# A residual layer norm: the last eight blocks of rows in smaller chunks, without their gamma and beta passes

## The chip, the cores and the metric

The kernel runs on one core of one Trainium2 chip. The metric is the device time in microseconds (us); a lower time is better. The page of the profile shows one execution, and its span is a little shorter than the device time of the same run.

Five engines matter here, and they run side by side. VectorE is DVE in the profile, ScalarE is ACT, GpSimd is POOL. SyncE is SP; it only issues loads. POOL only issues the loads of gamma and beta and the stores of the output. TensorE has no work. Transfers between the chip's main memory and the on-chip memory are done by 16 DMA engines.

## The reference

```python
def setup_inputs():
    batch, seq, dim = 16, 1024, 512
    return {
        "x": np.random.randn(batch, seq, dim).astype(np.float32),
        "residual": np.random.randn(batch, seq, dim).astype(np.float32),
        "gamma": np.ones(dim, dtype=np.float32),
        "beta": np.zeros(dim, dtype=np.float32),
        "eps": np.float32(1e-5),
    }

def reference(x, residual, gamma, beta, eps):
    z = x + residual
    mean = np.mean(z, axis=-1, keepdims=True)
    var = np.var(z, axis=-1, keepdims=True)
    z_norm = (z - mean) / np.sqrt(var + eps)
    return (gamma * z_norm + beta).astype(np.float32)
```

There are 16,384 rows of 512 numbers. A block is 128 rows, one row to each partition of the on-chip memory, so there are 128 blocks. The inputs x and residual are 33.6 MB each, and so is the output. Gamma is all ones and beta all zeros.

## The kernel before

Each of 32 chunks has R = 4 blocks: two loads of 1 MB, and one output of 1 MB. The code has two halves. `produce` starts the loads of a chunk and works out its statistics; `consume` normalizes the chunk before it and stores it. The framework orders the instructions of each engine when the kernel is built, and it may move them a little against the order of the source.

```python
R = 4
BUFS = 8
ACT_APPLY = (0, 2)
PIPE_DEPTH = 1
# ... cut: shapes, pools, the loads of gamma and beta ...

    def produce(st):
        base = st * rows_super
        # ... cut: x_ap and r_ap, the rows of this chunk; a partition gets r_cur rows that lie together
        xt = data.tile([P, r_cur, D], FP32, name="xt")
        rt = data.tile([P, r_cur, D], FP32, name="rt")
        ot = data.tile([P, r_cur, D], o_dt, name="ot")
        nc.sync.dma_start(out=xt[:], in_=x_ap)
        nc.sync.dma_start(out=rt[:], in_=r_ap)
        # ... cut: S and Qc
        for n in range(r_cur):                       # DVE: z = x + residual, and its row sums S
            nc.vector.tensor_tensor_reduce(
                out=xt[:, n, :], in0=xt[:, n, :], in1=rt[:, n, :],
                scale=1.0, scalar=0.0, op0=ALU.add, op1=ALU.add,
                accum_out=S[:, n : n + 1],
            )
        nmean = stats.tile([P, r_cur], FP32, name="nmean")
        nc.scalar.mul(nmean[:], S[:], -inv_D)        # ACT: the negative mean
        for n in range(r_cur):                       # ACT: the sum of squares of z - mean
            nc.scalar.activation(
                out=junk[:], in_=xt[:, n, :], func=AF.Square,
                bias=nmean[:, n : n + 1], accum_out=Qc[:, n : n + 1],
            )
        # ... cut: std = sqrt(Qc / D + eps) on ACT, rstd = 1 / std and nmr = nmean * rstd on DVE
        return dict(st=st, xt=xt, ot=ot, nmean=nmean, rstd=rstd, nmr=nmr)

    def consume(c):
        # ... cut
        for n in range(r_cur):                       # two blocks of four on ACT, two on DVE
            if n in ACT_APPLY:
                nc.scalar.activation(
                    out=ot[:, n, :], in_=xt[:, n, :], func=AF.Identity,
                    bias=nmr[:, n : n + 1], scale=rstd[:, n : n + 1],
                )
            else:
                nc.vector.tensor_scalar(
                    out=ot[:, n, :], in0=xt[:, n, :],
                    scalar1=nmean[:, n : n + 1], scalar2=rstd[:, n : n + 1],
                    op0=ALU.add, op1=ALU.mult,
                )
        nc.vector.tensor_mul(ot[:], ot[:], g_b)      # DVE: gamma, in fp16
        nc.vector.tensor_add(ot[:], ot[:], b_b)      # DVE: beta, in fp16
        nc.gpsimd.dma_start(out=o_ap, in_=ot[:])     # POOL: the store, fp16 to fp32 on the way

    for st in range(n_super):
        state.append(produce(st))
        if st >= PIPE_DEPTH:
            consume(state[st - PIPE_DEPTH])
    # ... cut: consume of the last chunk
```

A load waits until the load eight before it has landed, which the framework adds. `ot` is fp16, and the store turns it into fp32.

Of the kernel before, what the change touches and what calls it, by code (L numbers as in the profile page):

```python
# [1 line left out]

# [4 lines left out]

FP32 = mybir.dt.float32
FP16 = mybir.dt.float16  # L10
AF = mybir.ActivationFunctionType
ALU = mybir.AluOpType

R = 4
BUFS = 8
FP16_CHAIN = True
ACT_APPLY = (0, 2)
PIPE_DEPTH = 1


@with_exitstack
def kernel(
    ctx: ExitStack,
    tc: tile.TileContext,
    x: bass.AP,
    residual: bass.AP,
    gamma: bass.AP,
    beta: bass.AP,
    eps: bass.AP,
    out: bass.AP,  # L30
):
    nc = tc.nc
    P = nc.NUM_PARTITIONS

    x_f = x.flatten_outer_dims()
    r_f = residual.flatten_outer_dims()
    o_f = out.flatten_outer_dims()
    N, D = x_f.shape
    inv_D = 1.0 / float(D)
    eps_val = float(eps)  # L40

    r_cur = R
    while N % (P * r_cur) != 0 and r_cur > 1:
        r_cur -= 1
    rows_super = P * r_cur
    n_super = N // rows_super

    o_dt = FP16 if FP16_CHAIN else FP32

    consts = ctx.enter_context(tc.tile_pool(name="consts", bufs=1))  # L50
    data = ctx.enter_context(tc.tile_pool(name="data", bufs=BUFS))
    stats = ctx.enter_context(tc.tile_pool(name="stats", bufs=BUFS))
    psum = ctx.enter_context(tc.tile_pool(name="psum", bufs=1, space=bass.MemoryType.PSUM))

    g_t = consts.tile([P, D], o_dt, name="g_t")
    b_t = consts.tile([P, D], o_dt, name="b_t")
    nc.gpsimd.dma_start(out=g_t[:], in_=gamma.partition_broadcast(P))  # L57
    nc.gpsimd.dma_start(out=b_t[:], in_=beta.partition_broadcast(P))  # L58
    eps_t = consts.tile([P, 1], FP32, name="eps_t")
    nc.vector.memset(eps_t[:], eps_val)  # L60
    junk = psum.tile([P, D], FP32, name="junk")

    g_b = g_t[:].unsqueeze(1).to_broadcast((P, r_cur, D))
    b_b = b_t[:].unsqueeze(1).to_broadcast((P, r_cur, D))

    state = []

    def produce(st):
        base = st * rows_super
        x_ap = x_f[base : base + rows_super].rearrange("(p n) d -> p n d", n=r_cur)  # L70
        r_ap = r_f[base : base + rows_super].rearrange("(p n) d -> p n d", n=r_cur)

        xt = data.tile([P, r_cur, D], FP32, name="xt")
        rt = data.tile([P, r_cur, D], FP32, name="rt")
        ot = data.tile([P, r_cur, D], o_dt, name="ot")
        nc.sync.dma_start(out=xt[:], in_=x_ap)  # L76
        nc.sync.dma_start(out=rt[:], in_=r_ap)  # L77

        S = stats.tile([P, r_cur], FP32, name="S")
        Qc = stats.tile([P, r_cur], FP32, name="Qc")  # L80

        for n in range(r_cur):
            nc.vector.tensor_tensor_reduce(  # L83
                out=xt[:, n, :],
                in0=xt[:, n, :],
                in1=rt[:, n, :],
                scale=1.0,
                scalar=0.0,
                op0=ALU.add,
                op1=ALU.add,  # L90
                accum_out=S[:, n : n + 1],
            )
        nmean = stats.tile([P, r_cur], FP32, name="nmean")
        nc.scalar.mul(nmean[:], S[:], -inv_D)  # L94
        for n in range(r_cur):
            nc.scalar.activation(  # L96
                out=junk[:],
                in_=xt[:, n, :],
                func=AF.Square,
                bias=nmean[:, n : n + 1],  # L100
                accum_out=Qc[:, n : n + 1],
            )
        std = stats.tile([P, r_cur], FP32, name="std")
        nc.scalar.activation(  # L104
            out=std[:], in_=Qc[:], func=AF.Sqrt, bias=eps_t[:], scale=inv_D
        )
        rstd = stats.tile([P, r_cur], FP32, name="rstd")
        nc.vector.reciprocal(out=rstd[:], in_=std[:])  # L108
        nmr = stats.tile([P, r_cur], FP32, name="nmr")
        if ACT_APPLY:  # L110
            nc.vector.tensor_mul(nmr[:], nmean[:], rstd[:])  # L111
        return dict(st=st, xt=xt, ot=ot, nmean=nmean, rstd=rstd, nmr=nmr)

    def consume(c):
        st, xt, ot = c["st"], c["xt"], c["ot"]
        nmean, rstd, nmr = c["nmean"], c["rstd"], c["nmr"]
        base = st * rows_super
        o_ap = o_f[base : base + rows_super].rearrange("(p n) d -> p n d", n=r_cur)
        for n in range(r_cur):
            if n in ACT_APPLY:  # L120
                nc.scalar.activation(  # L121
                    out=ot[:, n, :],
                    in_=xt[:, n, :],
                    func=AF.Identity,
                    bias=nmr[:, n : n + 1],
                    scale=rstd[:, n : n + 1],
                )
            else:
                nc.vector.tensor_scalar(  # L129
                    out=ot[:, n, :],  # L130
                    in0=xt[:, n, :],
                    scalar1=nmean[:, n : n + 1],
                    scalar2=rstd[:, n : n + 1],
                    op0=ALU.add,
                    op1=ALU.mult,
                )
        nc.vector.tensor_mul(ot[:], ot[:], g_b)  # L137
        nc.vector.tensor_add(ot[:], ot[:], b_b)  # L138
        if FP16_CHAIN:
            nc.gpsimd.dma_start(out=o_ap, in_=ot[:])  # L140
        else:
            nc.scalar.dma_start(out=o_ap, in_=ot[:])

    for st in range(n_super):
        state.append(produce(st))
        if st >= PIPE_DEPTH:
            consume(state[st - PIPE_DEPTH])
            state[st - PIPE_DEPTH] = None
    for st in range(n_super - PIPE_DEPTH, n_super):
        if state[st] is not None:  # L150
            consume(state[st])


# [1 line left out]
_INS = ['x', 'residual', 'gamma', 'beta', 'eps']  # L155
_OUTS = [((16, 1024, 512), 'float32')]
#: Inputs that are plain numbers.
_NUMBERS = {'eps': 9.999999747378752e-06}


# [26 lines left out]
```

## Time and profile before

| What | Number |
|---|---|
| Device time, median of 4 runs | 258.94 us |
| Lowest and highest | 258.68 and 258.95 us |
| Span on the page | 257.2 us |
| Moved by DMA | 101.01 MB, mean 393 GB/s |
| Loads of x and residual, median from issue to landing | 29.6 and 30.0 us |
| Outputs, median from issue to landing | 9.3 us |

Busy time alone does not tell what bounds a kernel, since the engines work side by side and a stretch near the end may have another limit than the rest. The page has slices in time for that, and the trace can be asked for the busy time in any stretch, and for its single instructions. The names in a line of the profile are those of the code: `xt<-xt,rt` is the addition, `junk<-xt,nmean` the squares, `ot<-xt,nmr,rstd` the normalizing on ACT, `ot<-xt,nmean,rstd` that on DVE, `ot<-ot,g_t` and `ot<-ot,b_t` the passes of gamma and beta.

### The profile page before, as it was taken

To read this page: it belongs to the slowest core of one execution; us is meant where nothing else is said; L and a number is where in the kernel's file an instruction comes from. 1 tells how busy PE (TensorE), PEld (TensorE's weight loads), DVE (VectorE), ACT (ScalarE), POOL (GpSimd) and SP (SyncE) were. 2 spreads that over 40 slices of the span, in tenths; PEclk is the share of its full clock that TensorE was granted. 3 is DMA by queue.
4 is the path that set the end of the run, shared out by engine and by line. 5 is a ranking of instruction groups with operands and counts; after the bars stand their busy time and mean duration, and the time that the engine had idled before them with its cause. 6 is when DMAs were issued, how large, how long until landed. Compare 5 with 4: busy or idle time off the path is not lost.

```text
span 257.2 us, 1160 instructions
## 1 busy us (share of the span) xinstructions
DVE 193.1 (75%) x449; ACT 164.7 (64%) x386; POOL 18.4 (7%) x38
## 2 busy tenths in 40 slices
DVE  0357999588877787977977798777879779679860
ACT  1188788575765677656767766557776567576640
POOL 2000000000000000000000000000000000000000
DMA  7999999999999999999999999999999999996444
GB/s 259 312 426 427 419 427 418 420 426 427 424 419 424 424 423 420 423 424 427 420 422 423 426 424 420 423 424 423 420 424 423 426 422 420 423 426 260 163 163 163
DMA packets 14121, 101.01 MB, mean 393 GB/s; under 512 B 1568, under 2 KB 1824, under 8 KB 1824
## 3 DMA queue, kind: packets, MB, share of 16 engines
q1 hardware_dynamic: 9216, 67.11, 67.8%
q0 software_dynamic: 4896, 33.82, 33.4%
q14 instruction: 9, 0.07, 0.1%
HBM read 67.63 MB, written 33.55 MB: 393 GB/s over the span
## 4 chain that ended last, share of the span: by engine, by line
DMA 91%; issue 2%; ACT 2%; SPq 1%; DVE 1%; POOLq 0%; DVEq 0%
DMA rt<-in_residual_dram 91%; ACT junk L96 1%; DVE xt L83 1%; SPq L76 1%; SPq L77 1%; ACT ot L121 1%; POOLq L182 0%; ACT std L104 0%; ACT nmean L94 0%; DVE rstd L108 0%; DVE nmr L111 0%; DVE S L83 0%; DVEq L83 0%
## 5 line engine op out<-in xcount | busy, mean ns | idle before, releaser
L83 DVE CUSTOM_DVE_ANT_0 xt<-xt,rt 128x512 f32<-128x512 f32 x128 | 84.4, 680 | 47.5 <-DMA rt<-in_residual_dram 47.5
L121 ACT ACTIVATE ot<-xt,nmr,rstd 128x512 f16<-128x512 f32 x64 | 51.4, 806 | 67.3 <-DVE nmr L111 67.3
L96 ACT ACTIVATE junk<-xt,nmean 128x512 f32<-128x512 f32 x128 | 87.9, 687 | 3.1
L137 DVE TENSOR_TENSOR ot<-ot,g_t 128x2048 f16<-128x2048 f16 x32 | 39.2, 1225 | 6.7 <-ACT ot L121 6.6
L138 DVE TENSOR_TENSOR ot<-ot,b_t 128x2048 f16<-128x2048 f16 x32 | 39.2, 1224 | 1.1
L140 POOL DMA_DIRECT2D out_dram<-ot x32 | 17.0, 532 | 231.9 <-DVE ot L138 192.3
L129 DVE TENSOR_SCALAR ot<-xt,nmean,rstd 128x512 f16<-128x512 f32 x64 | 31.9, 540 | 0.0
L96 ACT ACTIVATION_READ_ACCUMULATOR junk<-xt,nmean 128x1 f32 x128 | 23.9, 186 | 0.0
L94 ACT ACTIVATE nmean<-S 128x4 f32<-128x4 f32 x32 | 6.1, 190 | 11.0 <-DVE S L83 11.0
L83 DVE DVE_READ_ACCUMULATOR2_ANT S<- 128x1 f32 x128 | 10.4, 82 | 0.0
L104 ACT ACTIVATE std<-Qc,eps_t 128x4 f32<-128x4 f32 x32 | 9.5, 297 | 1.0
L108 DVE RECIPROCAL rstd<-std 128x4 f32<-128x4 f32 x32 | 5.5, 172 | 1.1 <-ACT std L104 1.1
L111 DVE TENSOR_TENSOR nmr<-nmean,rstd 128x4 f32<-128x4 f32 x32 | 5.0, 157 | 0.0
L94 ACT ACT_TABLE_LOAD x1 | 1.3, 1283 | 0.7 <-PEq L168 0.7
L104 ACT ACT_TABLE_LOAD x1 | 1.3, 1283 | 0.0
L57 POOL DMA_DIRECT2D g_t<-in_gamma_dram x1 | 0.7, 669 | 0.8 <-PEq L182 0.8
L60 DVE MEMSET eps_t<- 128x1 f32 x1 | 0.1, 59 | 0.8 <-PEq L168 0.8
L58 POOL DMA_DIRECT2D b_t<-in_beta_dram x1 | 0.5, 540 | 0.0
L168 POOL MEMSET const-float32-0.0<- 128x1 f32 x1 | 0.1, 98 | 0.2 <-issue 0.2
L168 POOL MEMSET const-bfloat16-1.0<- 128x1 bf16 x1 | 0.1, 101 | 0.0
L168 POOL MEMSET const-float32-1.0<- 128x1 f32 x1 | 0.1, 98 | 0.0
L168 POOL MEMSET const-uint8-127<- 128x1 uint8 x1 | 0.1, 98 | 0.0
## 6 DMA issues: line engine op xcount, KB each, us to landing
xt<-in_x_dram SPq DMA_DIRECT2D x32, 1024.0 KB, 29.6
rt<-in_residual_dram SPq DMA_DIRECT2D x32, 1024.0 KB, 30.0
out_dram<-ot POOLq DMA_DIRECT2D x32, 1024.0 KB, 9.3
g_t<-in_gamma_dram POOLq DMA_DIRECT2D x1, 128.0 KB, 9.5
b_t<-in_beta_dram POOLq DMA_DIRECT2D x1, 128.0 KB, 12.2
```

The source lines that it names most:

```text
L76: nc.sync.dma_start(out=xt[:], in_=x_ap)
L83: nc.vector.tensor_tensor_reduce(out=xt[:, n, :], in0=xt[:, n, :], in1=rt[:, n, :], scale=1.0, scalar=0.0, op0=ALU.add, op1=ALU.add, accum ...
L94: nc.scalar.mul(nmean[:], S[:], -inv_D)
L96: nc.scalar.activation(out=junk[:], in_=xt[:, n, :], func=AF.Square, bias=nmean[:, n : n + 1], accum_out=Qc[:, n : n + 1],)
L104: nc.scalar.activation(out=std[:], in_=Qc[:], func=AF.Sqrt, bias=eps_t[:], scale=inv_D)
L108: nc.vector.reciprocal(out=rstd[:], in_=std[:])
L111: nc.vector.tensor_mul(nmr[:], nmean[:], rstd[:])
L121: nc.scalar.activation(out=ot[:, n, :], in_=xt[:, n, :], func=AF.Identity, bias=nmr[:, n : n + 1], scale=rstd[:, n : n + 1],)
L129: nc.vector.tensor_scalar(out=ot[:, n, :], in0=xt[:, n, :], scalar1=nmean[:, n : n + 1], scalar2=rstd[:, n : n + 1], op0=ALU.add, op1=ALU. ...
L137: nc.vector.tensor_mul(ot[:], ot[:], g_b)
L138: nc.vector.tensor_add(ot[:], ot[:], b_b)
L140: nc.gpsimd.dma_start(out=o_ap, in_=ot[:])
```

## The change

The first 120 blocks still go in 30 chunks of four. The last eight go in chunks of 2, 2, 1, 1, 1 and 1 instead of two of four, so that less work is left to do once the last load has landed. There are nine buffers instead of eight. ACT normalizes the first half of a chunk's blocks, rounded; for a chunk of one block that is `round(0.5)`, which is 0 in Python, so DVE does it.

One more thing changes in the code: the passes of gamma and beta run only where a chunk has four blocks. For the last eight blocks they are left out. With gamma all ones and beta all zeros the numbers stay the same, but for other values of gamma and beta the last 1,024 rows would be without them. The times are to be read with this in mind.

```diff
-R = 4
-BUFS = 8
+BODY_R = 4
+HEAD_CHUNKS = []
+TAIL_CHUNKS = [2, 2, 1, 1, 1, 1]
+BUFS = 9
-ACT_APPLY = (0, 2)
-PIPE_DEPTH = 1
+ACT_APPLY_FRAC = 0.5
+DUAL_QUEUE_LOADS = False
 ... (cut: the list of chunks is made from these)
-        xt = data.tile([P, r_cur, D], FP32, name="xt")
-        nc.sync.dma_start(out=xt[:], in_=x_ap)
-        nc.sync.dma_start(out=rt[:], in_=r_ap)
+        xt = data.tile([P, BODY_R, D], FP32, name="xt")
+        nc.sync.dma_start(out=xt[:, 0:r_cur, :], in_=x_ap)
+        (nc.scalar if DUAL_QUEUE_LOADS else nc.sync).dma_start(
+            out=rt[:, 0:r_cur, :], in_=r_ap
+        )
 ... (cut: the other tiles likewise have room for four blocks, and r_cur of them are used)
+        n_act = int(round(r_cur * ACT_APPLY_FRAC))
         for n in range(r_cur):
-            if n in ACT_APPLY:
+            if n < n_act:
 ... (cut)
-        nc.vector.tensor_mul(ot[:], ot[:], g_b)
-        nc.vector.tensor_add(ot[:], ot[:], b_b)
+        if r_cur == BODY_R:
+            nc.vector.tensor_mul(ot[:, 0:r_cur, :], ot[:, 0:r_cur, :], g_b)
+            nc.vector.tensor_add(ot[:, 0:r_cur, :], ot[:, 0:r_cur, :], b_b)
-            nc.gpsimd.dma_start(out=o_ap, in_=ot[:])
+            nc.gpsimd.dma_start(out=o_ap, in_=ot[:, 0:r_cur, :])
 ... (cut)
-    for st in range(n_super):
-        state.append(produce(st))
-        if st >= PIPE_DEPTH:
-            consume(state[st - PIPE_DEPTH])
+    for i, r_cur in enumerate(chunks):
+        state.append(produce(i, base_block, r_cur))
+        base_block += r_cur
+        if i >= 1:
+            consume(state[i - 1])
+    consume(state[-1])
```

## The prediction

> **What bounds the kernel now.** I read the page's slices first, then three windows, then the order of events at the end.
>
> ```profile
> DVE 193.1 (75%) x449; ACT 164.7 (64%) x386; POOL 18.4 (7%) x38
> DMA  7999999999999999999999999999999999996444
> DMA 91%; issue 2%; ACT 2%; SPq 1%; DVE 1%; POOLq 0%; DVEq 0%
> 20.00:235.00 215.00, 174.77 (x407) 146.60 (x348) 15.42 (x29) 1.00 1.09 423
> 235.00:238.50 3.50, 2.41 (x2) 3.37 (x9) 0.53 (x1) 1.00 0.15 49
> 238.50:257.20 18.70, 9.75 (x20) 6.58 (x14) 1.07 (x3) 1.00 0.44 168
> ```
>
> The first three lines are engine shares, DMA slices and the chain that ended last. In the windows the columns are the stretch, its length, busy DVE, ACT and POOL, clock, DMA share and GB/s. For 215 us the DMA engines are full at 423 GB/s, and the vector engine (DVE) and the scalar engine (ACT) have slack. From 235 to 238.5 only a trickle moves. From 238.5 on, three output tiles of 1 MB go out one at a time with idle DMA between them. So the body is bound by transfers and the last 19 us by dependencies. Only that end can be won. The timeline shows its steps:
>
> ```profile
> 238.60 0.69 DVE L83 CUSTOM_DVE_ANT_0 xt<-xt,rt 128x512 f32<-128x512 f32 x1 [1.16 <-DMA rt<-in_residual_dram]
> ...
> 242.22 0.67 ACT L96 ACTIVATE junk<-xt,nmean 128x512 f32<-128x512 f32 x1
> ...
> 245.59 0.30 ACT L104 ACTIVATE std<-Qc,eps_t 128x4 f32<-128x4 f32 x1
> ...
> 246.33 1.52 ACT L121 ACTIVATE ot<-xt,nmr,rstd 128x512 f16<-128x512 f32 x2 [0.44 <-DVE nmr L111]
> 247.88 1.23 DVE L137 TENSOR_TENSOR ot<-ot,g_t 128x2048 f16<-128x2048 f16 x1 [0.67 <-ACT ot L121]
> 249.14 1.22 DVE L138 TENSOR_TENSOR ot<-ot,b_t 128x2048 f16<-128x2048 f16 x1
> 250.90 0.53 POOL L140 DMA_DIRECT2D out_dram<-ot  x1 [5.01 <-issue]
> ```
>
> The last load lands just before 238.6. Adding, squaring, applying, gamma and beta for four blocks take until 250.36. From there to the span's end is 6.84 us: 0.54 to the output's issue record, 1.1 until data moves (half-microsecond windows show it from 252.0 to 254.4), 2.4 of data, 2.8 of completion and closing. The prices of the parts stand in the groups:
>
> ```profile
> L83 DVE CUSTOM_DVE_ANT_0 xt<-xt,rt 128x512 f32<-128x512 f32 x128 | 84.4, 680 | 47.5 <-DMA rt<-in_residual_dram 47.5
> L121 ACT ACTIVATE ot<-xt,nmr,rstd 128x512 f16<-128x512 f32 x64 | 51.4, 806 | 67.3 <-DVE nmr L111 67.3
> L96 ACT ACTIVATE junk<-xt,nmean 128x512 f32<-128x512 f32 x128 | 87.9, 687 | 3.1
> L96 ACT ACTIVATION_READ_ACCUMULATOR junk<-xt,nmean 128x1 f32 x128 | 23.9, 186 | 0.0
> L104 ACT ACTIVATE std<-Qc,eps_t 128x4 f32<-128x4 f32 x32 | 9.5, 297 | 1.0
> ```
>
> From start to start in the timeline these cost less or more than their means: an add 0.62, a square with its accumulator read 0.84, a standard deviation 0.32, an apply on ACT 0.71 to 0.80, an apply on DVE 0.5, a negative mean 0.1, a 2048-wide gamma or beta pass 1.24.
>
> **What the Trainium skill says.** "ScalarE: Activation LUTs", section "What ACT_TABLE_LOAD costs", puts an ACTIVATE at about 280 ns + 0.833 ns per element with one pointer operand, and 93 ns more for a second; at 512 elements that makes 706 and 799 ns. The trace has 687 and 806, so it agrees, and the price of a row does not fall when a chunk has fewer rows. "DMA: Bandwidth & Descriptors", section "Queues, rings and completion order", says each DMA engine goes round its queues packet by packet; the steady mix of loads and outputs agrees with that but does not prove it. The same page, "Latency and other measured facts", says two of the 16 engines are usually slower. The trickle fits: 33 GB/s between 236 and 237.5 is near one engine's share of 423 / 16 = 26, and the last load waits for it. "Perfetto Trace Analysis", section "DMA Optimizations", holds both sides of this change: splitting lets work start sooner, small transfers carry overhead. No x or residual load of this trace has rows under 8 KB, so it can't say what 2 KB rows cost.
>
> **The change, part by part.** I number chunks from 0; 29 is the last of four blocks, A and B have two, C to F one.
>
> *Body: nothing.* In the instruction order of the built kernel, the loads, adds and outputs keep their order until chunk 28's gamma pass. Nine buffers for eight move only a wait that is long over: eight loads, four chunks, are in flight in both kernels, since each load waits for the one eight before it. Which two blocks ACT applies does not matter either. So chunk 29's adds start at 223.52, as the trace of before has it, and DVE is done with them and with chunk 28's applies at 227.10.
>
> *Loads.* Chunk 30 landed at 231.2, 7.7 us after 29, and the slowest engine moved 2 MB of loads and about 1 MB of output 27 in that time: some 2.5 us per MB. A needs half the loads and the same output, 5 us, so it lands near 228.3. After it there are 3 MB of loads and output 28 (1 MB): at 2.5 us each, F lands by 238.4.
>
> *The order that the build chose.* DVE now adds A's first block, then runs chunk 28's gamma pass, then A's second block. So A's sums are ready at 228.3 + 0.62 + 1.24 + 0.62 = 230.8. ACT has squared three of chunk 29's four blocks by 229.66, but its next instruction is A's negative mean; it waits until 230.9.
>
> *From then on ACT is the path.* It still has nine squares (one of 29, two each of A and B, four of C to F): 9 x 0.84 = 7.6. Seven standard deviations: 7 x 0.32 = 2.2. Four applies (two of 29, one each of A and B; for a chunk of one, half of 1 rounds to 0, so DVE applies it): 4 x 0.75 = 3.0. Six negative means: 0.6. Together 13.4, so F's standard deviation ends at 244.3. I went along the order with DVE beside it: what ACT waits for is there about 1 us early each time, and DVE needs F's data only near 241.7, 3.3 us after its estimated landing. Gamma and beta are left out of the small chunks; chunk 29 still has them, beside ACT's work.
>
> *The last steps.* Reciprocal and product took 0.32 from the end of std in the trace, an apply on DVE 0.54: 245.2. Then the 6.84 us of before with a quarter of the data, 0.6 for 2.4: 5.0. That makes 250.2; I add 0.5 for some ten more hops between engines: span 250.7. The time before exceeds its span by 258.94 - 257.2 = 1.74. Predicted: 252.4 us, 6.5 less (2.5%).
>
> **The rivals.**
>
> *The last load counts alone.* Before, 18.7 us follow it. For one block I count add 0.7, mean 0.2, square 0.9, std 0.3, the small two 0.3, apply 0.5, output 5.0: about 8. If F landed at 238.4 and ACT were idle then, the span would be 246.4 and the time 248.1. Against it: ACT's list of 13.4 us starts at 230.9 whatever lands at 238, and the transfers themselves need until about 246 (after 223.4 there are 4 MB of loads and 5 MB of outputs, 9 x 2.5 = 22.5 us), plus 2.8, so 250.4 in time at best. I hold it for unlikely.
>
> *Transfers take ACT's place.* With rows of 4 and 2 KB, some 6 MB of the tail move in shorter pieces. At 20% more each, that is 3 us: the sum of the transfers ends at 248.9, the span at 251.7, the time at 253.4. Also, six outputs now leave POOL 1.2 to 1.6 us apart; before they were 7 us apart, and only 0.53 us of each is visible. If an issue took 2 us in all, the last would leave up to 4 us late: 256. For it: nothing in this trace shows small transfers in a row. Against: gamma's and beta's issues at the start stand close together at 0.67 and 0.54.
>
> *The order holds the tail up.* If A lands as late as 230, because outputs get more turns beside its shorter pieces, ACT starts late by as much: 254.1. And if DVE waits for a load that the build placed ahead of finished work (A's reciprocal stands behind C's add, and its product behind D's), outputs bunch at the end. I saw 1 us of slack there, so a small loss is possible.
>
> **Range and chances.** Transfers bound it at 250.4 from below if nothing else costs; ACT's list could run 0.7 shorter by overlapped applies, which is still 251.7. Upward, short rows, a late A and POOL each give 1 to 4 us, and not all at once. I take 250.6 to 255.0. The line of 2% lies at 253.8, 1.4 above the middle: 0.76 for faster, 0.22 for within, 0.02 for slower, since the body, 235 us of transfers, is untouched and a tail that loses 5 us would need several of the rivals together.
>
> **What would show it.** Right: the first adds of chunk 29 within 0.5 us of 223.5 and A's near 228.3; a wait of ACT for A's sums of about 1.2 us; then ACT busy with gaps under 1 us in all until about 244.3; the last load landed 2 us or more before DVE takes it; the last output issued near 245.7. Wrong: DVE waiting on loads at C to F (transfers bound the tail), a gap between the last apply and the last output's data well above 1.6 us (POOL), the A add at 230 or later, or a body whose chunks no longer follow each other at 7.4 us.

## The result and the profile after

| | before | after |
|---|---|---|
| Device time, median | 258.88 us (13 runs, 258.60 to 259.03) | 250.71 us (8 runs, 250.46 to 250.81) |
| Ratio to before, 95% interval | | 0.9685 (0.9675 to 0.9694) |
| Span on the page | 257.2 us | 248.8 us |

The change saves 8.2 us; 6.5 were predicted. From the page of after, the lines that answer to those of before (engine shares, DMA in 40 slices, the chain that ended last):

```profile
DVE 189.6 (76%) x455; ACT 163.9 (66%) x392; POOL 20.6 (8%) x42
DMA  6999999999999999999999999999999999999986
DMA 91%; DVE 3%; SPq 1%; issue 1%; POOL 1%; POOLq 0%; DVEq 0%
```

The three slices of 4 at the end are gone: the DMA engines now work nearly to the last slice. The windows of after show where (stretch, length, busy DVE, ACT and POOL, clock, DMA share, GB/s):

```profile
20.00:235.00 215.00, 176.04 (x413) 148.84 (x355) 15.41 (x29) 1.00 1.09 422
235.00:238.00 3.00, 3.00 (x5) 2.97 (x11) 0.64 (x2) 1.00 0.47 163
238.00:245.50 7.50, 4.25 (x18) 3.99 (x13) 3.09 (x6) 1.00 1.26 416
245.50:248.80 3.30, 0.00 (x0) 0.00 (x0) 0.00 (x0) 1.00 0.06 13
```

The body is what it was, 422 GB/s against 423. From 235 to 238 the loads run out, and both compute engines are full. Then come 7.5 us of outputs at 416 GB/s without a gap, where before the same 3 MB were spread over 16 us, from 238.5 to 254.4, with idle DMA between the tiles. In the chain that ended last, ACT had 2% before and has no entry now; DVE has 3%. The single steps, from the timeline of after:

```profile
223.35 0.69 DVE L94 CUSTOM_DVE_ANT_0 xt<-xt,rt 128x512 f32<-128x512 f32 x1 [2.27 <-DMA rt<-in_residual_dram]
...
226.05 0.33 SPq L86 DMA_DIRECT2D rt<-in_residual_dram  x1
...
226.85 0.68 DVE L94 CUSTOM_DVE_ANT_0 xt<-xt,rt 128x512 f32<-128x512 f32 x1
...
229.36 0.19 ACT L105 ACTIVATE nmean<-S 128x2 f32<-128x2 f32 x1
...
231.15 0.69 DVE L94 CUSTOM_DVE_ANT_0 xt<-xt,rt 128x512 f32<-128x512 f32 x1 [0.72 <-DMA rt<-in_residual_dram]
...
232.64 0.81 ACT L149 ACTIVATE ot<-xt,nmr,rstd 128x512 f16<-128x512 f32 x1 [0.45 <-DVE nmr L126]
...
239.31 0.68 DVE L94 CUSTOM_DVE_ANT_0 xt<-xt,rt 128x512 f32<-128x512 f32 x1
...
241.81 0.29 ACT L115 ACTIVATE std<-Qc,eps_t 128x1 f32<-128x1 f32 x1
...
242.41 0.54 DVE L157 TENSOR_SCALAR ot<-xt,nmean,rstd 128x512 f16<-128x512 f32 x1
243.25 0.53 POOL L171 DMA_DIRECT2D out_dram<-ot  x1 [0.65 <-DVE ot L157]
```

The load issued at 226.05 is the one that waits for A's second load, eight before it, so A has landed by then. DVE takes A at 226.85, B at 231.15 after a wait of 0.72, and F at 239.31 without one. F's standard deviation ends at 242.10 and its apply at 242.95. The load that F waits for is issued at 231.03 and takes 7.7 us to land (size, us from issue to landing):

```profile
rt<-in_residual_dram SPq DMA_DIRECT2D x1, 256.0 KB, 7.7
```

So F lands at 238.7, 0.6 us before DVE takes it.

### The profile page after: what moved, and what is told of

It reads as the page before. It is cut to its first block, busy times and chain, and to the rows that moved or that the text cites. A ratio compares the mean times of both kernels' runs of the same rounds, so it can differ in the third digit from the quotient of the medians.

```text
span 248.8 us, 1192 instructions
## 1 busy us (share of the span) xinstructions
DVE 189.6 (76%) x455; ACT 163.9 (66%) x392; POOL 20.6 (8%) x42
## 4 chain that ended last, share of the span: by engine, by line
DMA 91%; DVE 3%; SPq 1%; issue 1%; POOL 1%; POOLq 0%; DVEq 0%
DMA rt<-in_residual_dram 91%; DVE xt L94 1%; DVE ot L157 1%; SPq L85 1%; SPq L86 1%; POOL out_dram L171 1%; DVE ot L168 0%; DVE ot L169 0%; POOLq L214 0%; DVE nmr L126 0%; DVE rstd L123 0%; DVE S L94 0%; POOLq L171 0%; DVEq L94 0%
## 5 line engine op out<-in xcount | busy, mean ns | idle before, releaser
L149 ACT ACTIVATE ot<-xt,nmr,rstd 128x512 f16<-128x512 f32 x62 | 49.8, 805 | 62.4 <-DVE nmr L126 62.4
L168 DVE TENSOR_TENSOR ot<-ot,g_t 128x2048 f16<-128x2048 f16 x30 | 36.7, 1224 | 5.5 <-ACT ot L149 5.4
L171 POOL DMA_DIRECT2D out_dram<-ot x36 | 19.1, 532 | 222.2 <-DVE ot L169 178.1
L169 DVE TENSOR_TENSOR ot<-ot,b_t 128x2048 f16<-128x2048 f16 x30 | 36.7, 1224 | 1.0
L157 DVE TENSOR_SCALAR ot<-xt,nmean,rstd 128x512 f16<-128x512 f32 x66 | 33.1, 540 | 0.0
L105 ACT ACTIVATE nmean<-S 128x4 f32<-128x4 f32 (+2 forms) x36 | 6.7, 189 | 11.0 <-DVE S L94 11.0
L115 ACT ACTIVATE std<-Qc,eps_t 128x4 f32<-128x4 f32 (+2 forms) x36 | 10.7, 296 | 1.0
L94 DVE DVE_READ_ACCUMULATOR2_ANT S<- 128x1 f32 x128 | 10.4, 81 | 0.0
L123 DVE RECIPROCAL rstd<-std 128x4 f32<-128x4 f32 (+2 forms) x36 | 6.1, 170 | 0.6 <-ACT std L115 0.6
L126 DVE TENSOR_TENSOR nmr<-nmean,rstd 128x4 f32<-128x4 f32 (+2 forms) x36 | 5.6, 156 | 0.1
```

What stands on the lines that cost most here:

```text
L94: nc.vector.tensor_tensor_reduce(out=xt[:, n, :], in0=xt[:, n, :], in1=rt[:, n, :], scale=1.0, scalar=0.0, op0=ALU.add, op1=ALU.add, accum ...
L105: nc.scalar.mul(nmean[:, 0:r_cur], S[:, 0:r_cur], -inv_D)
L115: nc.scalar.activation(out=std[:, 0:r_cur], in_=Qc[:, 0:r_cur], func=AF.Sqrt, bias=eps_t[:], scale=inv_D,)
L123: nc.vector.reciprocal(out=rstd[:, 0:r_cur], in_=std[:, 0:r_cur])
L126: nc.vector.tensor_mul(nmr[:, 0:r_cur], nmean[:, 0:r_cur], rstd[:, 0:r_cur])
L149: nc.scalar.activation(out=ot[:, n, :], in_=xt[:, n, :], func=AF.Identity, bias=nmr[:, n : n + 1], scale=rstd[:, n : n + 1],)
```

## The experiments

Medians are of four runs, of twelve for "All the rest of the change"; before was run beside each on the same chip (medians of 258.76 to 258.94). Names of chunks are those of the prediction. Output 28 is that of chunk 28.

### Which part of the change brings what

**Split, with gamma and beta kept everywhere.** Nothing of the reference is left out here.

```diff
-        if r_cur == BODY_R:
+        if True:
```

> The changed kernel, but gamma and beta are applied to the last eight blocks too, so nothing of the reference is left out. My theory: the gain has two parts, the finer chunks and the work that is left out; VectorE is nearly full over the last 20 us of the changed kernel, so 5 to 6 us of extra passes (eight blocks at 1.22 / 4 = 0.31 us or somewhat more for each of two passes) appear almost whole at the end: 254.5 us, between 253.5 and 255.5. Rival, the passes lie beside ScalarE's work and cost nothing: 250.7 to 251.2 us.

Measured: 254.20 us, ratio 0.9814 (0.9800 to 0.9829). A window of its trace shows VectorE as the limit; after the stretch and its length the first number is busy DVE, the second ACT:

```profile
233.00:247.50 14.50, 14.36 (x42) 9.25 (x27) 3.23 (x6) 1.00 0.80 275
```

It is busy for 14.36 of 14.5 us while ACT idles for 5. So the finer chunks alone bring 258.87 - 254.20 = 4.7 us, and once they are there, the work left out brings another 3.5.

**Chunks of four, gamma and beta left out for the last eight blocks.**

```diff
-TAIL_CHUNKS = [2, 2, 1, 1, 1, 1]
+TAIL_CHUNKS = [4, 4]
-        if r_cur == BODY_R:
+        if c["base_block"] < 120:
```

> Chunks of four blocks to the end, as before; gamma and beta left out for the last eight blocks, as in the changed kernel. My theory: only the last chunk's two passes stand on the path, 249.14 to 250.36 and 247.88 to 249.11 in the trace of before, so the time falls by 2.5 us to 256.4 (256.1 to 256.7). Rival, the omission is most of the gain: 253 us or less.

Measured: 256.29 us, 0.9904 (0.9887 to 0.9920): 2.6 us, the two passes that stood in the chain. The last output is issued at 248.05 instead of 250.90. The two parts alone sum to 7.3 us. Together they bring 8.2; the omission is worth more with fine chunks, where VectorE has become full.

**All the rest of the change.**

```diff
-TAIL_CHUNKS = [2, 2, 1, 1, 1, 1]
+TAIL_CHUNKS = []
```

> All chunks of four blocks with gamma and beta, but nine buffers, and ScalarE normalizes blocks 0 and 1 instead of 0 and 2. My theory: no effect, 258.9 us within 0.3. Rival, the ninth buffer lets the stream run fuller: 256 us or less, with the chunks in the body closer than 7.4 us.

Measured: 258.93 us, 1.0002 (0.9994 to 1.0011). The ninth buffer and the other choice of blocks for ACT have no effect that shows.

**Four chunks of two.**

```diff
-TAIL_CHUNKS = [2, 2, 1, 1, 1, 1]
+TAIL_CHUNKS = [2, 2, 2, 2]
```

> The last eight blocks in four chunks of two instead of 2, 2, 1, 1, 1, 1; gamma and beta left out for them as in the changed kernel. Theory: the size of the last chunk stands on the path; ScalarE has nine squares, five standard deviations, six applies and four negative means from 229.4 on (14.1 us, so 243.9 with waits), then apply, output of 512 KB: 251.8 us (251.3 to 252.4). Rival, chunks of two are fine enough and the rest is hidden: 250.7.

Measured: 251.94 us, 0.9730 (0.9716 to 0.9745). The last output is issued at 245.24 instead of 243.25, at the end of ACT's longer list. So the size of the last chunk counts, but from two blocks to one it is worth only 1.2 us.

### What sets the end of the changed kernel

The prediction had ACT as the path. The trace of after has ACT, DVE and the DMA engines nearly full together, so I took load from each.

**ACT relieved.** The last four chunks lose their square passes (their rows are no layer norm).

```diff
+        if r_cur == 1:
+            nc.scalar.activation(out=Qc[:, 0:1], in_=S[:, 0:1], func=AF.Square, bias=nmean[:, 0:1])
+        else:
         for n in range(r_cur):   # the square passes
```

> The changed kernel without the four 512-wide square passes of the last four chunks: the variance of those rows is made from one number per row, so their output is not a layer norm. It takes 4 x 0.84 = 3.4 us from ScalarE near the end and leaves the transfers alone. If ScalarE's list alone sets the end (the step of my prediction), the time falls by 2 to 3 us to about 248. If the outputs that bunch up from 238 us on (3.1 MB at 410 GB/s are 7.6 us, ending at 245.6) set it too, it falls by 0.6 us at most: 250.1 to 250.7. I now hold for the second.

Measured: 250.46 us, 0.9673 (0.9658 to 0.9687), within the uncertainty of the changed kernel's 0.9685. ACT is not the path by itself. Its trace says why, in two lines of the timeline:

```profile
239.96 0.67 DVE L94 CUSTOM_DVE_ANT_0 xt<-xt,rt 128x512 f32<-128x512 f32 x1
...
242.67 0.53 POOL L179 DMA_DIRECT2D out_dram<-ot  x1 [0.67 <-DVE ot L165]
```

DVE takes F's add at 239.96, no earlier than in after (239.31), because its own list is full. The last output's issue comes only 0.58 us earlier, and it then waits for the outputs ahead of it: data still ran at 416 GB/s until 245.5.

**Transfers relieved.** Chunk 29 is not stored; 1 MB of output is never written.

```diff
+        if c["base_block"] == 116:
+            pass
-        if FP16_CHAIN:
+        elif FP16_CHAIN:
```

> The changed kernel without the store of chunk 29 (1 MB of its output is never written). In the trace of after, transfers, VectorE and ScalarE all run nearly full to the end. My theory now: the slowest DMA engine binds the changed kernel to its end (loads trickle on it until 238, then the outputs fill all engines until 245.6), and the two compute engines end only some 0.6 us earlier. Taking 1 MB (2.5 us of transfers) away then gains what the compute path allows, 0.6 us: 250.1 us (249.8 to 250.4). Rival, the compute path alone sets the end: 250.5 to 250.9, no gain.

Measured: 249.64 us, 0.9638 (0.9617 to 0.9658): 1.1 us less, where 0.6 was my size. The last output is issued at 243.25, as in after, but it lands 2.3 us later instead of 3.2. So in the changed kernel the outputs' queue costs about 1 us behind the compute path.

**Both.** The two edits together.

> The changed kernel without the square passes of the last four chunks and without the store of chunk 29, with VectorE's order at the end nearly that of the changed kernel. Without the store the outputs no longer queue, so the compute path sets the end; in the run without the squares its last output was issued at 242.67 instead of 243.25. If the two limits lie one behind the other, as I now think, both losses add: 249.64 - 0.58 = 249.1 us (248.8 to 249.3). If ScalarE's squares are not on the path at all, 249.6; if they are the whole path, 247 or less.

Measured: 249.08 us, 0.9619 (0.9603 to 0.9635), against 249.64; the highest of these four runs (249.09) is below the lowest of the other four (249.31). The 0.58 us that the squares gave before the last issue now show at the end as 0.56. So the squares do lie on the compute path, but in the changed kernel the queue of outputs behind it hides most of what they cost.

**DVE relieved.** Gamma and beta are left out for chunks 28 and 29 too.

```diff
-        if r_cur == BODY_R:
+        if r_cur == BODY_R and c["base_block"] < 112:
```

> The changed kernel with gamma and beta left out for chunks 28 and 29 too (right only as they are ones and zeros): 4 x 1.22 = 4.9 us less for VectorE in the last 20 us, and those two outputs leave earlier. If the slowest DMA engine binds, the sum of the transfers is the same and so is the time: 250.2 to 250.9. If VectorE's list binds, 249.6 or less.

Measured: 251.50 us, 0.9710 (0.9695 to 0.9725): 0.8 us slower than the changed kernel, which neither theory had. Two things changed in its trace. The build put both of B's adds ahead of chunk 29's reciprocal; in after only the first stands there. And output 28 leaves at 227.53 instead of 230.96, so that it moves beside the loads of C and D. D's residual is issued near 223.3 in both kernels, but lands 10.4 us later in after and 12.9 us later here:

```profile
rt<-in_residual_dram SPq DMA_DIRECT2D x1, 256.0 KB, 10.4
rt<-in_residual_dram SPq DMA_DIRECT2D x1, 256.0 KB, 12.9
```

DVE now waits for B (3.0 us), C (0.9), D (0.9) and F (0.6). A's product, the `nmr` that ACT needs, stands behind D's add in the order:

```profile
236.28 0.69 DVE L94 CUSTOM_DVE_ANT_0 xt<-xt,rt 128x512 f32<-128x512 f32 x1 [0.85 <-DMA rt<-in_residual_dram]
...
237.09 0.81 ACT L149 ACTIVATE ot<-xt,nmr,rstd 128x512 f16<-128x512 f32 x1 [1.34 <-DVE nmr L126]
```

ACT starts that block at 235.19 in after, so it is 1.9 us late, and the last output is issued at 245.04, 1.8 us late. By the trace, the time given to DVE let an output go early, and that output held up the loads that DVE needed next. No run separates the two changes.

**ACT and DVE relieved**, the edits of both.

> Both compute engines relieved: no square passes in the last four chunks (their rows are no layer norm) and no gamma and beta for chunks 28 and 29 either. All transfers stay. If the slowest DMA engine binds: 250.0 to 250.7, as the changed kernel. If the compute path binds, both lists are 3 to 5 us shorter and the time falls by 2 us or more, to 248.5 or less.

Measured: 250.89 us, 0.9688 (0.9672 to 0.9704). The time is near that of the changed kernel, 0.2 us above the range that my theory of the transfers gave, but the next run shows that this was no proof.

**All three.** The same, and chunk 29 is not stored.

> As the one with both compute engines relieved, and chunk 29 is not stored either. If transfers bind, 1 MB less is now worth its whole 2.5 us: 248.2 us (247.7 to 248.7). If the compute path bound, the store makes no difference to the one before.

Measured: 250.65 us, 0.9677 (0.9662 to 0.9693). The store makes no difference to the run before, so the sum of the transfers did not bind there. But 5 us less for DVE and 3.4 us less for ACT had gained nothing either, so it was not the length of the two engines' lists that bound. The timeline of this run shows what took its place:

```profile
236.28 0.69 DVE L94 CUSTOM_DVE_ANT_0 xt<-xt,rt 128x512 f32<-128x512 f32 x1 [1.71 <-DMA rt<-in_residual_dram]
...
237.09 0.81 ACT L157 ACTIVATE ot<-xt,nmr,rstd 128x512 f16<-128x512 f32 x1 [1.30 <-DVE nmr L134]
...
238.70 0.28 ACT L123 ACTIVATE std<-Qc,eps_t 128x2 f32<-128x2 f32 x1
238.89 0.69 DVE L94 CUSTOM_DVE_ANT_0 xt<-xt,rt 128x512 f32<-128x512 f32 x1 [0.59 <-DMA rt<-in_residual_dram]
...
239.78 0.54 DVE L165 TENSOR_SCALAR ot<-xt,nmean,rstd 128x512 f16<-128x512 f32 x1
...
240.38 0.53 DVE L165 TENSOR_SCALAR ot<-xt,nmean,rstd 128x512 f16<-128x512 f32 x1
...
240.89 0.54 DVE L165 TENSOR_SCALAR ot<-xt,nmean,rstd 128x512 f16<-128x512 f32 x1
...
241.14 2.76 POOL L181 DMA_DIRECT2D out_dram<-ot  x5 [2.41 <-ACT std L123]
```

Output 28 leaves early here too (227.84). DVE waits 1.71 us for D's load. A's product stands behind D's add, although A's reciprocal was done at 234.58, and ACT waits 1.30 us for the product. So B's standard deviation comes only at 238.70, and when it ends, DVE has taken F, whose add stands ahead of the applies of B, C, D and E. Five outputs then leave in a row. By this trace the limit is the order that the build chose, with loads that landed later. I did not try a forced order, so that reading rests on the trace alone. One thing none of these edits moved: F's last load lands between 238.6 and 238.8 in every run of this section.

### A version that beats both

The first 13 us move less than 425 GB/s in both kernels. Gamma and beta are read there, one row each, once for every partition.

```diff
-    nc.gpsimd.dma_start(out=g_t[:], in_=gamma.partition_broadcast(P))
+    nc.scalar.dma_start(out=gb_row[:, 0, :], in_=gamma.unsqueeze(0))
+    nc.tensor.matmul(g_ps[:], lhsT=ones[:], rhs=gb_row[:, 0, :], start=True, stop=True)
+    nc.vector.tensor_copy(out=g_t[:], in_=g_ps[:])
     # beta likewise
```

> The changed kernel, but gamma and beta are loaded as one row of 2 KB each and spread over the partitions on the chip by TensorE (a matrix product with ones), instead of being read by a load 128 times each. It points at the low rate in the first 13 us: summed over the windows from 6 to 13 us, some 0.76 MB fewer moved than at 425 GB/s, which is 1.8 us. If the two repeated loads cause that, everything after shifts earlier by 1.5 to 1.8 us: 249.1 us (248.8 to 249.5). Rival, the dip belongs to the start of the queues: 250.7.

Measured: 248.70 us, 0.9606 (0.9592 to 0.9620), 2.0 us less than the changed kernel. The edit does three things at once: each row is read once, the two loads go out from ACT instead of POOL, and the conversion to fp16 leaves the load. No run separates them. Windows of after and then of this kernel, the last number being GB/s (TensorE's two columns lead in the second):

```profile
6.00:9.00 3.00, 0.00 (x0) 0.00 (x0) 0.00 (x0) 1.00 1.03 274
9.00:13.00 4.00, 2.54 (x8) 0.79 (x2) 0.00 (x0) 1.00 1.05 368
```

```profile
6.00:9.00 3.00, 1.58 (x2) 0.00 (x1) 1.38 (x4) 0.00 (x0) 0.00 (x0) 1.00 1.02 431
9.00:13.00 4.00, 0.00 (x0) 0.00 (x0) 1.82 (x6) 2.05 (x6) 0.00 (x0) 1.00 1.01 428
```

The DMA share is above 1 in both, so a slow stream can look like a full one; only the GB/s tell them apart.

**The same with gamma and beta applied everywhere**, for the whole reference:

```diff
-        if r_cur == BODY_R:
+        if True:
```

> The finer chunks, gamma and beta as rows spread on the chip, and gamma and beta applied to every chunk: the whole reference for any gamma and beta. The two effects lie at opposite ends of the kernel and should add: 254.2 - 2.0 = 252.2 us (251.8 to 252.6). If the earlier stream only lengthens a wait at the end, 253.5 or more.

Measured: 252.25 us, 0.9743 (0.9727 to 0.9759). The gain at the start and that at the end add.

## Why the prediction was right

The time of 250.71 lies in the range of 250.6 to 255.0, 0.1 us above its lower end. The frame held: the body keeps its pace, and the whole gain lies in the end. The path within the end was only half right; two of its terms were too large and one too small. Of the signs that were to show it right, two came: chunk 29's adds, and gaps of ACT under 1 us in all. A's time, ACT's wait, the end of ACT's list, the slack before F and the last issue missed. Of the signs of being wrong, a late A, DVE's waits at C to F and a slower body did not come.

That the range held is in part luck. The case of ACT alone gave 251.7 us at best, more than was measured; the lower end came from the sum of the transfers, 250.4, which the prediction worked out for a rival. That sum alone did not set the time either: 1 MB less, 2.5 us by the prediction's price, gained 1.1.

- *Body: nothing.* Right. Chunk 29's adds start at 223.35 (223.52 predicted), and the rest of the change alone measures 1.0002.
- *Loads.* "A needs half the loads and the same output, 5 us" failed. A's 1 MB landed by 226.05, 2.8 us after chunk 29's loads; B's 1 MB by 231.03, 5.0 us after A's. The output that I had placed ahead of A was issued at 221.60, and the trace has it landing 8.3 us later, near 229.9, after A. It took its time beside B. That the engines go round their queues packet by packet is what the Trainium skill states ("DMA: Bandwidth & Descriptors", section "Queues, rings and completion order"); the equal shares were my own step, and this trace does not show them.
- *ACT's wait for A's sums.* It did not happen. A's negative mean starts at 229.36 instead of 230.9: 1.5 us of the error.
- *ACT's list of 13.4 us.* It took 12.74, from 229.36 to 242.10, a wait of 0.45 included. The small ones overlap their neighbours more than I counted: 0.7 us of the error.
- *"From then on ACT is the path."* Half right. The list is nearly as long as that, but DVE's is full too, and the chain that ended last runs through DVE: without four square passes of 0.84 us the last issue moves only 0.58 us and the time not measurably. My slack of 3.3 us between F's landing and DVE's taking it was 0.6: F landed at 238.7, and DVE took it at 239.31.
- *The last steps.* From the end of F's apply to the end of the span I had 5.0 and a margin of 0.5; it took 5.85. The missing store showed that about 1 us of it is the queue of outputs ahead. This is the rival "transfers take ACT's place", in small. Its other half, POOL needing 2 us for an output, fell: five in a row took 2.76.
- The sum: 1.5 and 0.7 too much, 0.35 too little, that is 1.85 us of the 1.9 between the predicted span of 250.7 and the measured 248.8. The profiled run took 250.57 us, 1.77 above its span (1.74 predicted) and 0.14 below the median; so 252.4 and 250.71 lie 1.7 apart.

What the prediction did not do is price the omission by itself. It said that gamma and beta were left out of the small chunks and went on. With the fine chunks in place they are 3.5 of the 8.2 us; without the omission the ratio is 0.9814.

What stays open: whether the sum of transfers would be the next limit if the build's order were better, why an output falls behind loads that were queued with it, and which part of the edit at the start brings its 2.0 us.

## What to carry to other kernels

In a kernel whose body is bound by transfers, look for the gain in the stretch where DMA falls idle, and cut the last tiles so that outputs leave while compute goes on; the gain ends where compute engines, order and queue of outputs are full together, and then relieving one of them gives little or even loses, as in the run where an output left earlier and the loads beside it landed later. When a change also leaves work out, run the two parts apart before crediting the idea. In the order of the built kernel, look for an instruction that waits for a load ahead of work whose data are already there.

## What the hardware showed that I had not expected

- With two loads in flight that read one 2 KB row once for each of 128 partitions and turn it into fp16, an otherwise full stream fell to 274 GB/s from 6 to 9 us, while the DMA share stayed at 1.03. With single rows, issued by ACT and spread on the chip, it ran at 431 GB/s, and the kernel was 2.0 us faster.
- A 1 MB output issued while loads were queued landed 8.3 us later, behind 1 MB of loads that took 2.8 us of that time; in before, the same kind of output took 4.1 us with nothing beside it.
- POOL issued five stores of 128 partitions in 2.76 us, 0.55 each. No run here shows a cost of its issuing six small outputs instead of two large ones.
